# Lower parts of the down-projection weights: one subtraction on VectorE, or a negated copy on ScalarE and an accumulating DMA

## The chip, the cores and the metric

The kernel is one program on one core of a Trainium2 chip. The metric is device microseconds of one execution. The kernel before takes 2463.43 us (median of 3 runs, 2463.13 to 2463.51).

## The reference

Two transformer blocks are computed on the same 512 tokens of width 1024, in float32. The first block has windowed attention and neighbourhood attention side by side, gates, an output projection, and a feed-forward part of width 4096:

```python
h2 = rms_norm(x, norm_mlp[l])
x = x + jnp.square(jax.nn.relu(h2 @ w_up[l])) @ w_down[l]
```

The second block has two layers. Each holds a gated feed-forward part of width 2816, an attention and short-convolution mixer, and a second gated feed-forward part:

```python
def swiglu(h, w_gate, w_up, w_down):
    return (jax.nn.silu(h @ w_gate) * (h @ w_up)) @ w_down
x = x + 0.5 * swiglu(rms_norm_2(x, ffn1_norm[l]), ffn1_wg[l], ffn1_wu[l], ffn1_wd[l])
...
x = x + 0.5 * swiglu(rms_norm_2(x, ffn2_norm[l]), ffn2_wg[l], ffn2_wu[l], ffn2_wd[l])
```

So there are five feed-forward parts: `mlp`, and `ffn1` and `ffn2` of either layer. Each has a down projection (`w_down`, `ffn1_wd`, `ffn2_wd`).

## The kernel before

**Split operands.** Activations are held transposed: 8 tiles of 128 features by 512 tokens. To keep float32 accuracy with TensorE's float32r operands, every matrix is held as an upper part (rounded to float32r) and a lower part (what the rounding left). A product is three matmuls: upper weight by upper activation, upper by lower, lower by upper (lines 450 to 452 for the down projections).

**Weights.** All weights lie in HBM as one stream in the order in which they are used. SyncE loads it in units of up to 1024 columns (512 KB, line 333) into 5 buffers `raw`. The stream is cut into 1282 items. An item is what TensorE needs for one step: at most 128x512 of a weight. `split_item` (line 357) makes an item's two parts: ScalarE writes the upper part `wh` (line 376, CAST), VectorE subtracts it from the raw weight into the lower part `wl` (line 378). Both come from rings of 7 buffers. An item is split five items (`AHEAD`) before the matmuls that use it, in program order, so ScalarE's and VectorE's queues hold these splits between the work on the results of the steps before. When the last item of a unit is split, the next load is put into SyncE's queue; it waits for the last reader of the old unit.

**Feed-forward parts.** `ffn_order` writes out the order. The hidden features are cut into slices (six for `mlp`, of 4, 4, 6, 6, 6 and 6 blocks of 128; four for the others, of 4, 6, 5 and 7). Up projections are steps "P" (seven products of 256 columns, Strassen's scheme, lines 1082 to 1084; their items are a whole 128x512, some of them sums of raw weights made by VectorE at line 355) or "R" (plain, lines 1120 to 1122). Down projections are steps "D" (slice, output block n, part 0 or 1): 16 for each slice. The D steps of one slice stand between the P steps of the next one; those of the last slice stand alone at the end. A D item has the columns of half a slice: 256 (two blocks), 384 (three) or 512 (four). All 352 D items: 96 in `mlp` (32 of 256, 64 of 384), and 64 in each of the other four (24 of 256, 32 of 384, 8 of 512), together 128 of 256, 192 of 384 and 32 of 512.

**After the last D step of an output block** VectorE adds the result to the residual (line 897) and prepares the next part's operands: in `prep_pairs` (line 613) and `squares` (line 572) ScalarE and VectorE take turns, and the next output block queues behind.

**Other queues.** GpSimd's queue issues a few DMAs: constants, 12 bias tables of 384 KB in the attention stage, 8 tiles of 256 KB of the input (line 1037), the last at 325 us.

The items and the split:

Of the kernel before, what the change touches and what calls it, by code (L numbers as in the profile page):

```python
# [9 lines left out]
F32 = mybir.dt.float32  # L10
F32R = mybir.dt.float32r
AF = mybir.ActivationFunctionType
ALU = mybir.AluOpType
# [5 lines left out]
D = 1024  # L19
# [212 lines left out]
def two_blocks(ctx, tc, plan, xT, wstream, vecs, sinks, rpb_g, dists, masks, outT):  # L232
    nc = tc.nc
# [75 lines left out]
    for i in range(4):  # L309
        s = slot[7 * i:7 * i + 7]  # L310
        lo, hi = slice(0, H), slice(H, S)
# [12 lines left out]
    def load_unit():  # L324
        u = st["unit"]
        if u >= len(units):
            return
        st["unit"] += 1
        w = sum(len(b[2]) for b in units[u])
        r = raw_p.tile([P, UNIT], F32, tag="raw", name=f"raw{u}")  # L330
        src = wstream[st["off"]: st["off"] + P * w].rearrange("(p f) -> p f", p=P)
        st["off"] += P * w
        nc.sync.dma_start(r[:, :w], src)
        raw[u] = r

    def parts_of(key, part):
        nk = len(blocks[key][2]) // P
        h = nk // 2
        return (0, h) if part == 0 else (h, nk)

    def combine(idx):

        if idx >= len(items) or idx in combined:
            return
        combined.add(idx)
        key, part = items[idx]
        if key[1:2] == ("P",) and part in (6, 7, 3):
            ra, rb = raw[where[key][0][0]], raw[where[key][1][0]]
            a11, a12, a21, a22 = ra[:, :S], ra[:, S:], rb[:, :S], rb[:, S:]
            new = sums_of.setdefault(key, {})  # L350
            for name, p, q, op in {6: (("s1", a21, a22, ALU.add), ("s2", "s1", a11, ALU.subtract)),
                                   7: (("s3", a11, a21, ALU.subtract),), 3: (("s4", a12, "s2", ALU.subtract),)}[part]:
                new[name] = t = big("t", f"{name}_{idx}")[:, :S]
                p, q = (new[v] if isinstance(v, str) else v for v in (p, q))
                nc.vector.tensor_tensor(t, p, q, op)  # L355

    def split_item(idx):
        key, part = items[idx]
        combine(idx)
        h = wt_p.tile([P, S], F32R, tag="wh", name=f"wh{idx}")  # L360
        lo = wt_p.tile([P, S], F32R, tag="wl", name=f"wl{idx}")
        if blocks[key][0] is not None:
            (u, off), = where[key]
            k0, k1 = parts_of(key, part)
            src = raw[u][:, off + P * k0:off + P * k1]
        else:
            ra, rb = raw[where[key][0][0]], raw[where[key][1][0]]
            new = sums_of.get(key, {})
            if key[1] == "R":
                src = (ra, rb)[part % 2][:, S * (part // 2):S * (part // 2) + S]  # L370
            else:
                src = {1: ra[:, :S], 2: ra[:, S:], 4: rb[:, S:]}.get(part)
                if src is None:
                    src = new[{5: "s1", 6: "s2", 7: "s3", 3: "s4"}[part]]
        w = src.shape[1]
        nc.scalar.copy(h[:, :w], src)  # L376
        combine(idx + 1)
        nc.vector.tensor_tensor(lo[:, :w], src, h[:, :w].bitcast(F32), ALU.subtract)  # L378
        ready[idx] = (h, lo)
        for u, _ in where[key]:  # L380
            uses[u] -= 1
            if uses[u] == 0:
                raw.pop(u)
                freed.append(u)
        while freed and min(freed) == st["oldest"]:
            freed.remove(st["oldest"])
            st["oldest"] += 1
            load_unit()
# [4 lines left out]
    def split_to(idx):  # L393
        oldest = min(live) if live else st["next"]
        idx = min(idx, oldest + RING - 1, len(items) - 1)
        while st["split"] <= idx:
            split_item(st["split"])
            st["split"] += 1
# [150 lines left out]
    def big(tag, name):  # L549
        return at_p.tile([P, 768], F32, tag=tag, name=name)  # L550
# [880 lines left out]
```

## Time and profile before

| | |
|---|---|
| median of 3 runs | 2463.43 us |
| the profiled execution: its time, its span | 2464.76 us, 2463.0 us |
| TensorE (PE) busy | 2436.1 us, 99% |
| VectorE (DVE) busy | 1960.7 us, 80% |
| ScalarE (ACT) busy | 1261.0 us, 51% |
| GpSimd (POOL) busy | 24.6 us, 1% |
| DMA, share of 16 engines taken by the weight queue | 29.0% |

How to read it: the span is what lies between the first and the last instruction, and the time of the run is 1.8 us more. PE is TensorE's matmuls, whose ends are modelled, so that busy time shows gaps but not the speed inside it. DVE, ACT and POOL are VectorE, ScalarE and GpSimd; SP is SyncE, which only issues DMAs. An instruction's idle time in brackets names what released it.

### The profile page before, as it was taken

The page shows a single profiled execution, that of the slowest core. Times are in us where ns is not written, and L with a number is a line of the kernel's source. Part 1 is how long each engine was busy: PE and PEld are TensorE (multiplying, and loading weights), DVE is VectorE, ACT ScalarE, POOL GpSimd, SP SyncE. Part 2 cuts the span into 40 slices and gives each one's busy share as a digit, 9 for nine tenths or more (in the row PEclk, how much of TensorE's full clock was granted, in tenths as well). Part 3 has the DMA queues.
Part 4 walks back from the last instruction along what each step waited for, and adds up shares of the span by engine and source line. Part 5 has one row for each costly group of instructions (what it writes and reads, how often), then busy time and mean ns, then how long its engine had stood idle before and what let it go on. Part 6 is the DMA issues. An engine that isn't in the chain of part 4 may idle for free.

```text
span 2463.0 us, 39488 instructions
## 1 busy us (share of the span) xinstructions
PE 2436.1 (99%) x15098; PEld 2167.0 (88%) x15098; DVE 1960.7 (80%) x3943; ACT 1261.0 (51%) x2744; POOL 24.6 (1%) x37
## 2 busy tenths in 40 slices
PE   8999999999999999999999999999999999999998
PEld 6888888999879999988899999899999878999997
DVE  7778678877679878768798888898887687988885
ACT  5554355544455545544565445665445455654454
POOL 2000000000000000000000000000000000000000
PEclk9999999999999999999999999999999999999999
DMA  4222432233322332332223323323333322233332
GB/s 161 69 92 88 118 114 82 94 101 100 106 85 91 101 115 88 114 95 69 84 80 103 107 99 101 102 93 112 98 104 106 102 69 77 75 107 108 106 94 79
DMA packets 73901, 239.45 MB, mean 97 GB/s; under 512 B 8320, under 2 KB 10384, under 8 KB 73712
## 3 DMA queue, kind: packets, MB, share of 16 engines
q1 hardware_dynamic: 70496, 228.10, 29.0%
q0 software_dynamic: 1776, 7.27, 1.0%
q8 instruction: 118, 1.93, 0.3%
q10 hardware_dynamic: 1440, 1.57, 0.2%
q14 instruction: 71, 0.58, 0.1%
HBM read 234.81 MB, written 2.10 MB: 96 GB/s over the span
## 4 chain that ended last, share of the span: by engine, by line
PE 93%; DVE 5%; ACT 1%; issue 0%; DMA 0%; SPq 0%; DVEq 0%; ACTq 0%
PE X L1084 7%; PE X L1083 7%; PE X L1082 7%; PE YZ L1082 5%; PE YZ L1083 5%; PE YZ L1084 5%; PE mlp_D L451 2%; PE mlp_D L450 2%; PE mlp_D L452 2%; PE 0, 'ffn2'_D L450 2%; PE 1, 'ffn1'_D L450 2%; PE 0, 'ffn1'_D L450 2%; PE 0, 'ffn1'_D L451 2%; PE 0, 'ffn2'_D L451 2%; PE 1, 'ffn1'_D L451 2%; PE 0, 'ffn1'_D L452 2%
## 5 line engine op out<-in xcount | busy, mean ns | idle before, releaser
L378 DVE TENSOR_TENSOR wl<-raw,wh 128x512 fp32r<-128x512 f32 (+2 forms) x890 | 531.7, 609 | 98.3 <-ACT wh L376 91.4
L376 ACT CAST wh<-raw 128x512 fp32r<-128x512 f32 (+2 forms) x890 | 469.6, 555 | 8.4 <-DMA raw<-in_w 2.6
L1082 PE MATMUL X<-r,wh 128*128 128x256 f32 x1568 | 445.2, 284 | 3.8 <-ACT g L1088 3.6
L1084 PE MATMUL X<-r,wl 128*128 128x256 f32 x1568 | 444.0, 283 | 0.0
L1083 PE MATMUL X<-r,wh 128*128 128x256 f32 x1568 | 443.9, 283 | 0.0
L376 ACT CAST wh<-s 128x512 fp32r<-128x512 f32 x392 | 242.7, 620 | 224.6 <-DVE s L355 219.2
L1082 PE MATMUL YZ<-r,wh 128*128 128x256 f32 x1176 | 334.4, 284 | 0.8 <-ACT u L1094 0.8
L1083 PE MATMUL YZ<-r,wh 128*128 128x256 f32 x1176 | 333.3, 283 | 0.0
L1084 PE MATMUL YZ<-r,wl 128*128 128x256 f32 x1176 | 333.2, 283 | 0.0
L378 DVE TENSOR_TENSOR wl<-s,wh 128x512 fp32r<-128x512 f32 x392 | 268.8, 686 | 69.5 <-ACT wh L376 67.6
L1082 PEld LDWEIGHTS X<-r,wh 128*128 128x128 f32 x1568 | 300.1, 191 | 15.2 <-ACT g L1088 4.0
L1083 PEld LDWEIGHTS X<-r,wh 128*128 128x128 f32 x1568 | 300.1, 191 | 10.3 <-issue 1.2
L1084 PEld LDWEIGHTS X<-r,wl 128*128 128x128 f32 x1568 | 300.2, 191 | 0.0
L1082 PEld LDWEIGHTS YZ<-r,wh 128*128 128x128 f32 x1176 | 226.3, 192 | 1.6 <-ACT u L1094 1.4
L1083 PEld LDWEIGHTS YZ<-r,wh 128*128 128x128 f32 x1176 | 226.3, 192 | 0.2 <-issue 0.2
L1084 PEld LDWEIGHTS YZ<-r,wl 128*128 128x128 f32 x1176 | 226.3, 192 | 0.0
L1096 ACT COPY g<-X 128x256 f32<-128x256 f32 x98 | 36.5, 372 | 141.6 <-PE X L1084 141.5
L1097 DVE TENSOR_TENSOR u<-u,g 128x256 f32<-128x256 f32 x98 | 41.6, 424 | 75.8 <-ACT g L1096 75.8
L450 PE MATMUL mlp_D<-r,wh 128*128 128x512 f32 x256 | 100.1, 391 | 0.0
L451 PE MATMUL mlp_D<-r,wh 128*128 128x512 f32 x256 | 100.1, 391 | 0.0
L452 PE MATMUL mlp_D<-r,wl 128*128 128x512 f32 x256 | 99.6, 389 | 0.0
L1092 ACT COPY u<-X 128x256 f32<-128x256 f32 x98 | 36.5, 373 | 101.0 <-PE X L1084 101.0
(429 smaller groups left out, 5258.9 us busy)
## 6 DMA issues: line engine op xcount, KB each, us to landing
raw<-in_w SPq DMA_DIRECT2D x320, 512.0 KB, 3.7
raw<-in_w SPq DMA_DIRECT2D x64, 384.0 KB, 3.5
raw<-in_w SPq DMA_DIRECT2D x32, 448.0 KB, 3.5
raw<-in_w SPq DMA_DIRECT2D x32, 320.0 KB, 2.9
raw<-in_w SPq DMA_DIRECT2D x28, 256.0 KB, 2.6
bb<-in_rpb POOLq DMA_DIRECT2D x12, 384.0 KB, 3.3
xt<-in_x POOLq DMA_DIRECT2D x8, 256.0 KB, 2.9
xt<-in_x SPq DMA_DIRECT2D x1, 1024.0 KB, 12.7
```

Of the source, the lines that this page charges most:

```text
L376: nc.scalar.copy(h[:, :w], src)
L378: nc.vector.tensor_tensor(lo[:, :w], src, h[:, :w].bitcast(F32), ALU.subtract)
L450: nc.tensor.matmul(self.ps, h[:, c], hx, start=(self.n == 1), stop=False)
L451: nc.tensor.matmul(self.ps, h[:, c], lx, start=False, stop=False)
L452: nc.tensor.matmul(self.ps, lo[:, c], hx, start=False, stop=end)
L1082: nc.tensor.matmul(out, h[:, c], hx, start=first, stop=False, skip_group_check=skip)
L1083: nc.tensor.matmul(out, h[:, c], lx, start=False, stop=False, skip_group_check=skip)
L1084: nc.tensor.matmul(out, l[:, c], hx, start=False, stop=(k == 3), skip_group_check=skip)
L1092: nc.scalar.copy(u[:, lo], out)
L1096: nc.scalar.copy(g[:, hi], out)
L1097: nc.vector.tensor_tensor(u[:, hi], u[:, hi], g[:, hi], ALU.add)
```

## The change

For the items of down projections alone, the lower part is made in another way. ScalarE, behind its cast, writes the negative of the upper part into `wl` (an ACTIVATE with Copy and the scale -1). Then a DMA issued by GpSimd adds the raw weight to it in place, element by element. VectorE's subtraction of these 352 items is gone. All other items are split as before.

```diff
         w = src.shape[1]
         nc.scalar.copy(h[:, :w], src)
-        combine(idx + 1)
-        nc.vector.tensor_tensor(lo[:, :w], src, h[:, :w].bitcast(F32), ALU.subtract)
+        if key[1:2] == ("D",):
+
+            nc.scalar.activation(lo[:, :w], h[:, :w].bitcast(F32), AF.Copy, scale=-1.0)
+            nc.gpsimd.dma_start(lo[:, :w].bitcast(F32), src, accum_op=ALU.add)
+            combine(idx + 1)
+        else:
+            combine(idx + 1)
+            nc.vector.tensor_tensor(lo[:, :w], src, h[:, :w].bitcast(F32), ALU.subtract)
```

Line numbers behind the change are larger by 6.

**First place: the first slice of `mlp`, around item 144** (output block 4, part 0; `wh144` and `wl144` are its parts, `X6` and `g4`, `u4` belong to the up projection between). ScalarE's queue before, then now, then GpSimd's queue now:

```order
L376 CAST wh143_4061<-raw64_4016 128x256
L1259 ACTIVATE g4_3881<-g4_3881 128x512
L1260 ACTIVATE u4_3882<-u4_3882 128x512
L376 CAST wh144_4089<-raw64_4016 128x256
L1088 COPY g6_4098<-X6_4097 128x256
L553 CAST r36_124<-g4_3881 128x512
```

```order
L376 CAST wh143_4068<-raw64_4022 128x256
L379 ACTIVATE wl143_4069<-wh143_4068 128x256
L1265 ACTIVATE g4_3882<-g4_3882 128x512
L1266 ACTIVATE u4_3883<-u4_3883 128x512
L376 CAST wh144_4097<-raw64_4022 128x256
L379 ACTIVATE wl144_4098<-wh144_4097 128x256
L1094 COPY g6_4107<-X6_4106 128x256
L559 CAST r36_124<-g4_3882 128x512
```

```order
L380 DMA wl142_4058<-raw64_4022 128x256
L380 DMA wl143_4069<-raw64_4022 128x256
L380 DMA wl144_4098<-raw64_4022 128x256
L380 DMA wl147_4152<-raw64_4022 128x256
L380 DMA wl148_4163<-raw65_4024 128x256
```

Every D cast on ScalarE is followed by a negated copy, ahead of the copies out of PSUM, and GpSimd's queue holds nothing but the accumulating transfers.

**Second place: the end of `mlp`, where its last D items are split between the preparation of the next part** (`xt` is the residual, `mlp_D_5_2` the last slice's result of output block 2, `sqa`, `sqf` the squares). VectorE's queue before and now:

```order
L586 TENSOR_TENSOR inv_140<-inv_140,sqa4_7147 128x512
L586 TENSOR_TENSOR r32_7062<-r32_7062,sqf4_7151 128x512
L378 TENSOR_TENSOR wl317_7156<-raw125_6956,wh317_7155 128x384
L378 TENSOR_TENSOR wl318_7171<-raw127_7025,wh318_7170 128x384
L897 SCALAR_TENSOR_TENSOR xt_87<-mlp_D_5_2_7108,xt_87 128x512
L627 TENSOR_TENSOR xg2_7184<-xt_87 128x256
```

```order
L592 TENSOR_TENSOR inv_140<-inv_140,sqa4_7239 128x512
L592 TENSOR_TENSOR r32_7150<-r32_7150,sqf4_7243 128x512
L903 SCALAR_TENSOR_TENSOR xt_87<-mlp_D_5_2_7198,xt_87 128x512
L633 TENSOR_TENSOR xg2_7278<-xt_87 128x256
```

ScalarE's queue at the same place, before and now:

```order
L577 ACTIVATE sqf4_7151<-xt_87 128x512
L376 CAST wh317_7155<-raw125_6956 128x384
L376 CAST wh318_7170<-raw127_7025 128x384
L626 ACTIVATE r14_102<-xt_87,gfg_153 128x256
L628 ACTIVATE r14_102<-xg2_7184,gfg_153 128x256
```

```order
L583 ACTIVATE sqf4_7243<-xt_87 128x512
L376 CAST wh317_7247<-raw125_7039 128x384
L379 ACTIVATE wl317_7248<-wh317_7247 128x384
L376 CAST wh318_7263<-raw127_7112 128x384
L379 ACTIVATE wl318_7264<-wh318_7263 128x384
L632 ACTIVATE r14_102<-xt_87,gfg_153 128x256
```

The pair of subtractions between two output blocks is gone from VectorE, and ScalarE has four instructions there for two.

## Rows read from the trace of the kernel before

**Rows 1.** The page's first part: busy us, share of the span, instructions.
```profile
PE 2436.1 (99%) x15098; PEld 2167.0 (88%) x15098; DVE 1960.7 (80%) x3943; ACT 1261.0 (51%) x2744; POOL 24.6 (1%) x37
```

**Rows 2.** PE's waits, whole span: us in total, times, longest.
```profile
PE R L1120 <- ACT r L1125: 4.0, 1, 4.0
PE X L1082 <- ACT g L1088: 3.6, 2, 2.8
```

**Rows 3.** Groups by form: count, busy us, mean ns, idle before and releaser.
```profile
L378 DVE TENSOR_TENSOR wl<-raw,wh 128x384 fp32r<-128x384 f32 x192 | 105.3, 553 | 32.3 <-ACT wh L376 32.3
L378 DVE TENSOR_TENSOR wl<-raw,wh 128x256 fp32r<-128x256 f32 x160 | 66.3, 418 | 11.0 <-ACT wh L376 10.5
L376 ACT CAST wh<-raw 128x512 fp32r<-128x512 f32 x538 | 322.1, 617 | 2.7 <-DMA raw<-in_w 2.6
...
L376 ACT CAST wh<-raw 128x384 fp32r<-128x384 f32 x192 | 95.8, 511 | 4.2 <-PE 1, 'ffn2'_D L451 1.0 <-PE 0, 'ffn1'_D L451 1.0 <-PE 1, 'ffn1'_D L451 1.0
L376 ACT CAST wh<-raw 128x256 fp32r<-128x256 f32 x160 | 62.8, 403 | 1.5 <-PE mlp_D L452 1.1 <-PE mlp_D L451 0.4
...
L577 ACT ACTIVATE sqa<-xt 128x512 f32<-128x512 f32 x36 | 22.3, 618 | 7.3 <-DVE xt L897 7.3
```

**Rows 4.** GpSimd's loads: KB and median us to landing, extremes, one issue and its releaser.
```profile
bb<-in_rpb POOLq DMA_DIRECT2D x12, 384.0 KB, 3.3
xt<-in_x POOLq DMA_DIRECT2D x8, 256.0 KB, 2.9
...
DMA to landing us min/median/max: 3.1/3.3/4.2
...
271.08 0.69 DVE L1036 TENSOR_TENSOR gb<-xt,gb 128x512 f32<-128x512 f32 x1
...
272.07 0.54 POOL L1037 DMA_DIRECT2D xt<-in_x  x1 [49.47 <-DVE gb L1036]
```

**Rows 5.** Timeline: start us, us, instruction; three D casts, each with its first lower matmul.
```profile
409.12 0.39 ACT L376 CAST wh<-raw 128x256 fp32r<-128x256 f32 x1
...
413.07 0.39 PE L452 MATMUL mlp_D<-r,wl 128*128 128x512 f32 x1
...
838.02 0.41 ACT L376 CAST wh<-raw 128x256 fp32r<-128x256 f32 x1
...
843.72 0.39 PE L452 MATMUL 0, 'ffn1'_D<-r,wl 128*128 128x512 f32 x1
...
2319.08 0.51 ACT L376 CAST wh<-raw 128x384 fp32r<-128x384 f32 x1
...
2324.26 0.39 PE L452 MATMUL 1, 'ffn2'_D<-r,wl 128*128 128x512 f32 x1
```

**Rows 6.** Timeline, end of `mlp`: the pairs of subtractions; ScalarE between.
```profile
687.79 1.02 DVE L378 TENSOR_TENSOR wl<-raw,wh 128x384 fp32r<-128x384 f32 x2
693.44 1.02 DVE L378 TENSOR_TENSOR wl<-raw,wh 128x384 fp32r<-128x384 f32 x2
...
698.72 1.02 DVE L378 TENSOR_TENSOR wl<-raw,wh 128x384 fp32r<-128x384 f32 x2
...
697.90 0.91 ACT L376 CAST wh<-raw 128x384 fp32r<-128x384 f32 x2
700.37 0.72 ACT L637 ACTIVATE r<-xt,gfg 128x512 fp32r<-128x512 f32 x1 [1.56 <-DVE xt L897]
```

**Rows 7.** Two of PE's stalls, and stretches behind them: busy by engine, PEclk, DMA.
```profile
714.77 0.80 PE L1120 MATMUL R<-r,wh 128*128 128x512 f32 x1 [4.04 <-ACT r L1125]
...
714.70:721.60 6.90, 6.83 (x17) 5.39 (x18) 6.83 (x12) 4.99 (x11) 0.00 (x0) 0.54 0.00 0
...
391.49 0.39 PE L1082 MATMUL X<-r,wh 128*128 128x256 f32 x1 [0.79 <-ACT g L1088]
...
391.40:400.00 8.60, 8.51 (x54) 7.79 (x55) 7.00 (x15) 4.91 (x13) 0.00 (x0) 1.00 0.24 81
```

## The prediction

> **What bounds the kernel now.** I read the page's first part, then TensorE's waits over the whole span, then the costliest groups by form, and last the timeline around down projections. The first part shows PE busy for 2436.1 of 2463.0 us, VectorE for 1960.7 and ScalarE for 1261.0 [rows 1]. A PE at 99% leaves 27 us that a faster VectorE could give back. PE's waits say where they are: no row names the lower weights `wl`, so VectorE's subtractions are in time everywhere. What is worth having is two stalls behind ScalarE: 4.0 us once on the R steps, at the change from `mlp` to `ffn1`, and 3.6 us in two waits on a copy out of PSUM [rows 2]; the rest lies at the start and the end of the program, where no down item is split. So the kernel is bound by TensorE in its D and P steps, and by the exchange between VectorE and ScalarE only at the end of `mlp`.
>
> **What goes.** 352 subtractions: 128 of 256 columns by 418 ns, 192 of 384 by 553 ns [rows 3], and 32 of 512 by some 690 ns (the same 135 ns more for 128 columns more): 53.5 + 106.2 + 22.1 = 182 us of VectorE, 7% of the span. Since TensorE doesn't wait for them, this is worth nothing in itself, except at the end of `mlp`. There three pairs of 1.02 us stand ahead of the next residual add [rows 6], some 0.95 us each until the add starts. The end of `mlp` is a chain: VectorE's add releases ScalarE's preparation, which sat idle 1.56 us for it [rows 6], ScalarE's results release VectorE, and the copy that TensorE waited 4.04 us for is in ScalarE's queue behind all of it [rows 7]. Without the pairs VectorE is 3 x 0.95 = 2.9 us earlier. ScalarE gets six negated copies there, two between two blocks, 2 x 0.51 = 1.0 us by the cast of the same width [rows 3], and they fit into the 1.56 us that it sat idle. But once the adds come earlier it has only about 1.56 - 0.95 = 0.6 us for these 1.0, so it takes back up to 0.4 us a block in the two blocks that follow at once. I take 2.5 us off the stall, which leaves 1.5.
>
> Behind that stall the granted clock was 0.54 for 6.9 us, the lower of its two levels (1.2 of 2.4 GHz) for most of it; PE had stood idle for 4.04 us before it fell. Behind a stall of 0.79 us at 391 it stayed at 1.00 [rows 7]. The low stretch costs 6.9 x 0.46 = 3.2 us. A stall of 1.5 us lies between the two, nearer to the short one, and I take the 3.2 us as given back, with two chances in three.
>
> **What comes on ScalarE.** 352 negated copies. The trace has no activation with a constant scale on these shapes; the nearest, a Square of 512 columns, takes 618 ns where the cast takes 617 [rows 3], so I price them as casts: 128 x 403 + 192 x 511 + 32 x 617 = 169 us, which raises ScalarE from 1261 to 1430 us, 58%. That is beside the matmuls. It can't be a gain, and at worst each copy out of PSUM behind one comes 0.4 to 0.5 us later; TensorE waited for such a copy only twice outside the R steps [rows 2]; the longer wait, 2.8 us, is at the start of `ffn1`, with no D item near. At the other, at 391 [rows 7], a D cast and its copy are now in the queue ahead, and I put 0.5 us there.
>
> **What comes on GpSimd and the DMA engines.** 352 accumulating transfers, 128 of 128 KB, 192 of 192 KB, 32 of 256 KB. One issue took 0.54 us, and started 0.30 us behind the end of the VectorE instruction that released it (272.07 - 271.77) [rows 4]; 190 us of GpSimd, which has nothing else to do. No accumulating transfer is in the trace. From issue to landing GpSimd's loads of 256 KB took 2.9 us and of 384 KB 3.3 us, up to 4.2 [rows 4], so 128 KB more are 0.4 us more. An accumulation reads the raw weights and the destination: twice the bytes. Lower bound: the doubled reads cost nothing, 2.5 us for 128 KB. Upper bound: reading and adding are two passes, one behind the other, 5.0 us for 128 KB and 5.4 for 192. I take the bytes read as what counts, and so the rows for 256 and 384 KB themselves: 2.9 us for 256 columns, 3.3 for 384, 3.7 for 512.
>
> The Trainium skill (Collectives: The Full Stack, "The bandwidth ceiling: the fold count and why AG ≠ RS ≠ AR") says of a reduction in the DMA path that the add itself is free and only its second source read costs, halving the rate. Taken so, the sum is mine; the trace has no accumulation to show it, so it settles nothing about the upper bound.
>
> **Is it in time?** The lead is from the end of a D cast to the first lower matmul of its item. At the tight place it is 413.07 - 409.51 = 3.56 us, at an ordinary one 843.72 - 838.43 = 5.29, and for 384 columns 2324.26 - 2319.59 = 4.67 [rows 5]. Against them stand the negated copy, the start of the issue and the transfer: 0.40 + 0.30 + 2.9 = 3.6 us for 256 columns, 0.51 + 0.30 + 3.3 = 4.1 for 384. So the ordinary places are in time by 1.7 and 0.6 us, and the tightest is level. The tight ones come at the start of a slice. I put 1 us in all for the handful that miss. At the end of `mlp` the casts at 697.90 are later than elsewhere, and TensorE may wait 1 to 2 us there, but it then waits less for ScalarE at 714: no cost.
>
> One more wait is added: the load into a raw buffer (SyncE's queue, in order) now waits for the transfer's landing rather than for the subtraction, some 3 us later for units that D items end. Everything behind it on that queue moves too. The cover is the five buffers: casts lost only 2.6 us to loads in the whole run [rows 3]. I cost it at nothing; without cover it would take from the lead.
>
> The Trainium skill (SBUF — State Buffer, "Who interferes with whom") states that GpSimd's making of descriptors can be blocked by VectorE in its two-port modes, and infers that two-input operations don't block it. By the rule's strict reading each issue would wait for a VectorE operation of 0.4 to 0.7 us, which puts the tight places out of time; no row here shows an issue beside such an operation.
>
> **Sum.** Against the profiled execution (2464.76 us, span 2463.0): - 2.5 (stall) - 3.2 (clock) + 0.5 (copy) + 1.0 (tight places) = - 4.2 us, so 2460.6; the median of the runs shown is 1.3 us below that execution, which gives 2459.3, say 2459.5.
>
> **Rivals.**
> *Tight places pay.* If a transfer takes 4.2 us, the longest of GpSimd's loads [rows 4], the tight place misses by 0.40 + 0.30 + 4.2 - 3.56 = 1.3 us and the 384-column one by 5.0 - 4.67 = 0.3, while the ordinary one still holds by 0.4. 272 D items stand between P steps (five slices of `mlp`, three of each other part, 16 each); if one in eight pays 0.4 us, that is 14 us, less the 4 to be had: 2473. For it: engines shared with weight loads that take 29% of them (the table of the profile), and VectorE at 80% beside the issues. Against it: half of the 384 KB loads landed within 3.3 us.
> *The transfer is two passes, and TensorE waits for it.* At 5.0 and 5.4 us the tight place misses by 2.1 us, the ordinary by 0.4, the 384-column one by 1.5. A miss pushes TensorE back, not ScalarE's casts already done, so the next four or five items have that much more lead: one item in five pays, 272 / 5 = 54, by about 1 us: 2463.4 + 54 = 2517. From some 3.5 us for 128 KB on the loss outweighs the gain. For it: nothing in the trace has an addition in a transfer. Against it: reads can run beside each other, with 16 engines 29% busy.
> *Hidden, and nothing comes back.* ScalarE takes VectorE's place as the pace at the end of `mlp` (its copies are in the chain), the stall stays, the clock falls: 2463.5.
>
> **How the numbers follow.** Forecast 0.50, tight places 0.18, two passes 0.20, nothing 0.12. A measurement of this kernel tells about 0.2% (4.9 us) from no change, so faster means below 2458.5. The forecast's own range is 2456 (the whole 4.0 us and the clock) to 2462 (the stall without the clock); two fifths of its chance are below 2458.5: 0.20, and 0.30 of no change. Tight places give 0.05 of no change and 0.13 of slower, two passes 0.20 of slower, nothing 0.12 of no change. With that, faster 0.20, same 0.45, slower 0.35, of which I move 0.02 to slower for the unknown issue cost of an accumulation. The range is 2456 to 2505: it takes in the tight places and the cheaper half of the two passes.
>
> **What would show it.** Right: no PE wait on a GpSimd transfer outside the starts of slices; transfers of 2.9 to 3.7 us from issue to landing; the 4.04 us wait on L1125 at 1.5 us or less, and no stretch of clock 0.54 behind it; VectorE near 1779 us busy, ScalarE near 1430. Wrong: PE waits named after `wl` all over the D steps, or casts waiting for raw loads. A landing of 4 us or more for 128 KB would make the sign wrong.

## The result and the profile after

The changed kernel takes 2542.51 us (2540.64 to 2550.96, four runs) where the kernel before takes 2463.47 us (2463.13 to 2464.25): a ratio of 1.0327, interval 1.0304 to 1.0350. I had forecast 2459.5 us, in a range from 2456 to 2505. It is slower by 79 us, and outside the range. The profiled execution took 2550.96 us (span 2549.2), 86.2 us of span more than the profiled one of before. Executions differ by their mean granted clock: the four of the kernel after go from 2540.64 us at 0.995 to 2550.96 at 0.991, and of 21 of the kernel before ten at 0.996 took 2463.64 to 2464.98 us and five at 0.998 2462.65 to 2462.81, so both profiled executions are of the slower kind.

The page's first part of the kernel after, as [rows 1]:

```profile
PE 2465.6 (97%) x15098; PEld 2174.1 (85%) x15098; DVE 1819.9 (71%) x3591; ACT 1423.2 (56%) x3096; POOL 331.7 (13%) x389
```

VectorE lost 141 us of work and ScalarE gained 162. PE runs the same 15098 matmuls. Its idle time (span less busy) rose from 26.9 us [rows 1] to 83.6, by 56.7; its busy time rose by 29.5.

PE's waits of the kernel after (us in total, times, longest), as [rows 2], say what it waits for:

```profile
PE 0, 'ffn2'_D L458 <- DMA wl<-raw: 13.9, 9, 2.4
PE 1, 'ffn2'_D L458 <- DMA wl<-raw: 13.2, 8, 2.4
PE 0, 'ffn1'_D L458 <- DMA wl<-raw: 12.7, 9, 2.6
PE 1, 'ffn1'_D L458 <- DMA wl<-raw: 12.0, 10, 2.2
...
PE mlp_D L458 <- DMA wl<-raw: 6.4, 8, 2.2
PE X L1088 <- ACT g L1094: 4.1, 2, 2.8
...
PE R L1126 <- ACT r L1131: 0.9, 2, 0.5
```

The five rows on `wl` are new: 58.2 us in 44 waits, spread over all five parts. The wait on the R steps fell from 4.0 to 0.9 us. So the term that I counted as a gain came, and is buried under a wait that I had priced at 1 us.

The new instructions on the page (count, busy us, mean ns, idle before), the transfers by size with KB and median us from issue to landing, and two lines of the answer on the transfer's line (an issue in ns, then landings in us: least, median, most):

```profile
L380 POOL DMA_DIRECT2D wl<-raw x352 | 306.7, 877 | 1893.6 <-ACT g L1094 647.3
...
L376 ACT CAST wh<-raw 128x512 fp32r<-128x512 f32 (+2 forms) x890 | 474.9, 554 | 8.9 <-DMA raw<-in_w 8.0
...
L379 ACT ACTIVATE wl<-wh 128x256 fp32r<-128x256 f32 (+2 forms) x352 | 174.6, 496 | 11.2
...
wl<-raw POOLq DMA_DIRECT2D x192, 192.0 KB, 3.7
...
wl<-raw POOLq DMA_DIRECT2D x128, 128.0 KB, 2.9
...
wl<-raw POOLq DMA_DIRECT2D x32, 256.0 KB, 4.7
...
L380 POOL DMA_DIRECT2D wl<-raw x352: 860/869/1174, 391.6 to 2524.7; - x176
...
DMA to landing us min/median/max: 2.6/3.7/8.0
```

For 128 KB the median is the one I took (2.9); for 192 and 256 KB it is 0.4 and 1.0 us above mine (3.3, 3.7); the longest is 8.0. The median hides two populations, which the timeline shows. Here is a late transfer of 128 KB in `ffn2` (start us, us, instruction, [idle before <- releaser]; SyncE's row covers two weight loads, issued at 1316.93 and 1318.32):

```profile
1316.87 0.40 ACT L376 CAST wh<-raw 128x256 fp32r<-128x256 f32 x1
...
1316.93 1.71 SPq L333 DMA_DIRECT2D raw<-in_w  x2
...
1317.30 0.42 ACT L379 ACTIVATE wl<-wh 128x256 fp32r<-128x256 f32 x1
...
1318.01 0.87 POOL L380 DMA_DIRECT2D wl<-raw  x1 [4.11 <-ACT u L1100]
...
1321.14 0.40 PE L457 MATMUL 0, 'ffn2'_D<-r,wh 128*128 128x512 f32 x1
...
1323.95 0.50 PE L458 MATMUL 0, 'ffn2'_D<-r,wl 128*128 128x512 f32 x1 [2.41 <-DMA wl<-raw]
```

The cast ended at 1317.27, and PE was ready for the lower weights at 1323.95 - 2.41 = 1321.54: a lead of 4.3 us. The negated copy (0.42) and the start of the issue (1318.01 - 1317.72 = 0.29) are as predicted, and with 2.9 us more all would have been in time by 0.6. But the transfer took 5.9 us. One weight load of 512 KB had been issued 1.1 us before it, and another came 0.3 us behind it. What the DMA engines did meanwhile (queue: packets, MB, share of 16 engines; q1 carries the weight loads, q0 the transfers) in 1317.5 to 1320.5, then 1320.5 to 1322.5, and last, for a transfer issued at 1726.31 with no load beside it, in 1725.5 to 1729.5:

```profile
q1 hardware_dynamic: 174, 0.65, 75.7%
q0 software_dynamic: 12, 0.01, 2.5%
...
q1 hardware_dynamic: 104, 0.39, 55.2%
q0 software_dynamic: 116, 0.11, 35.0%
...
q0 software_dynamic: 144, 0.13, 22.6%
q1 hardware_dynamic: 4, 0.00, 0.1%
...
wl<-raw POOLq DMA_DIRECT2D x1, 128.0 KB, 2.7
```

At 1320.5, 2.5 us behind the issue at 1318.01, the engines had started 12 of the transfer's 144 packets, and the loads took 75.7% of the engines. The transfer's other packets went by turns with the second load's, until 1323. The transfer alone had its first packet 1.4 us behind its issue and had started all 144 by 2.5 us; they took 22.6% of 4 us, 0.9 us, and the landing came at 2.7.

Sorted by whether a weight load could be under way beside it (either counted from 1.7 us behind its issue to its landing), the 352 transfers fall into two groups: 145 without one have a median of 2.98 us (most 4.61), 207 with one a median of 4.71, a quarter over 5.8 and the longest 8.04. This split is worked out from the records of issue and landing; counted from 1.3 us it gives medians of 2.87 and 4.44. The packets' records, taken in the queue's order, show two parts of the delay: those with a load beside have their first packet 2.43 us behind the issue in the median, the others 1.44, and from the first packet to the last it is 1.57 us for 1.19. So such a transfer both starts later and is stretched.

The idle time has a second price. Stretches of the kernel after (busy by engine, PEclk, DMA share, GB/s): behind the stall above, the stretch after that, and the end of `mlp` with the two waits on the R steps in it, where [rows 7] has a clock of 0.54:

```profile
1325.00:1328.40 3.40, 3.40 (x18) 3.40 (x17) 1.30 (x3) 0.00 (x0) 0.00 (x0) 0.51 0.42 151
1328.40:1332.00 3.60, 3.60 (x27) 3.38 (x27) 2.30 (x6) 2.43 (x6) 0.52 (x1) 1.00 0.00 0
...
720.00:735.00 15.00, 13.61 (x57) 10.29 (x57) 14.33 (x26) 10.24 (x21) 0.00 (x0) 1.00 0.34 109
```

For 3.4 us PE is at the lower of its two levels (1.2 of 2.4 GHz) although it has work throughout. There are eleven such new stretches, each behind a wait on `wl` of 1.75 to 2.6 us, while the one at 714 is gone (three waits of 1.78, 2.35 and 2.36 us have none behind them). The mean granted clock of the whole span went from 0.996 to 0.991: 0.009 x 2549.2 - 0.004 x 2463.0 = 13 us. Set against the kernel before matmul by matmul, from start to start (worked out from the timeline), the 86 us of span are 65 at the 44 waits on `wl`, 14 net in stretches of low clock, and 9 at the matmuls just behind the waits and in other D steps, less 2 to 3 at the stalls that both kernels have. The first matmul behind a wait takes 0.50 us for 0.39.

### The profile page after: what moved, and what is told of

Read it like the earlier page. It is cut to its first block, busy times and chain, and to the rows that moved or that the text cites. A ratio compares the mean times of both kernels' runs of the same rounds, so it can differ in the third digit from the quotient of the medians.

```text
span 2549.2 us, 40496 instructions
## 1 busy us (share of the span) xinstructions
PE 2465.6 (97%) x15098; PEld 2174.1 (85%) x15098; DVE 1819.9 (71%) x3591; ACT 1423.2 (56%) x3096; POOL 331.7 (13%) x389
## 3 DMA queue, kind: packets, MB, share of 16 engines
q0 software_dynamic: 52464, 70.20, 16.3%
q10 hardware_dynamic: 1440, 1.57, 0.2%
## 4 chain that ended last, share of the span: by engine, by line
PE 73%; DMA 11%; issue 10%; DVE 2%; ACT 2%; POOL 1%; POOLq 0%; SPq 0%; DVEq 0%; ACTq 0%
DMA wl<-raw 11%; PE X L1088 5%; PE X L1090 5%; PE X L1089 5%; PE YZ L1088 3%; PE YZ L1090 3%; PE YZ L1089 3%; PE 0, 'ffn1'_D L458 1%; PE mlp_D L458 1%; PE 1, 'ffn1'_D L458 1%; PE 0, 'ffn2'_D L458 1%; PE 1, 'ffn2'_D L458 1%; PE 0, 'ffn1'_D L456 1%; PE 0, 'ffn1'_D L457 1%; PE 1, 'ffn1'_D L456 1%
## 5 line engine op out<-in xcount | busy, mean ns | idle before, releaser
L380 POOL DMA_DIRECT2D wl<-raw x352 | 306.7, 877 | 1893.6 <-ACT g L1094 647.3
L376 ACT CAST wh<-raw 128x512 fp32r<-128x512 f32 (+2 forms) x890 | 474.9, 554 | 8.9 <-DMA raw<-in_w 8.0
L384 DVE TENSOR_TENSOR wl<-raw,wh 128x512 fp32r<-128x512 f32 (+1 forms) x538 | 355.0, 671 | 54.4 <-ACT wh L376 48.0
L1088 PEld LDWEIGHTS X<-r,wh 128*128 128x128 f32 x1568 | 304.5, 194 | 16.6 <-ACT g L1094 4.6
L1089 PEld LDWEIGHTS X<-r,wh 128*128 128x128 f32 x1568 | 304.3, 194 | 11.0 <-issue 1.2
L379 ACT ACTIVATE wl<-wh 128x256 fp32r<-128x256 f32 (+2 forms) x352 | 174.6, 496 | 11.2
L1094 ACT COPY g<-X 128x256 f32<-128x256 f32 x98 | 36.3, 370 | 170.7 <-PE X L1090 170.7
L1102 ACT COPY g<-X 128x256 f32<-128x256 f32 x98 | 36.5, 372 | 133.3 <-PE X L1090 133.2
L457 PE MATMUL mlp_D<-r,wh 128*128 128x512 f32 x256 | 100.9, 394 | 0.5 <-DVE r L560 0.5
```

Source lines behind the costliest of these rows:

```text
L379: nc.scalar.activation(lo[:, :w], h[:, :w].bitcast(F32), AF.Copy, scale=-1.0)
L380: nc.gpsimd.dma_start(lo[:, :w].bitcast(F32), src, accum_op=ALU.add)
L457: nc.tensor.matmul(self.ps, h[:, c], lx, start=False, stop=False)
L1088: nc.tensor.matmul(out, h[:, c], hx, start=first, stop=False, skip_group_check=skip)
L1089: nc.tensor.matmul(out, h[:, c], lx, start=False, stop=False, skip_group_check=skip)
L1094: nc.scalar.copy(g[:, lo], out)
```

## Experiments

Theory 1: the transfers land late because weight loads are under way on the same engines. Theory 1a: a load's packets that are already queued are served first; theory 1b: the packets of the two take turns. Theory 2: the addition itself makes them slow, whatever is beside them. Theory 3: ScalarE's added copies push work back. The run named "The end of `mlp` alone" asks whether the predicted gain there is real.

**VectorE adds in place of the transfer.** ScalarE's copies stay, GpSimd's transfers go.

```diff
-            nc.gpsimd.dma_start(lo[:, :w].bitcast(F32), src, accum_op=ALU.add)
+            nc.vector.tensor_tensor(lo[:, :w], src, lo[:, :w].bitcast(F32), ALU.add)
```

> All 352 down items keep ScalarE's negated copy, and VectorE adds the raw weight to it (a two-input operation as long as the subtraction was), so there is no accumulating transfer. Theory 1 (the transfers land late because they queue on the 16 DMA engines behind weight loads) and theory 2 (an accumulation takes long by itself) both expect no wait on the lower weights and 2463 to 2467 us: ScalarE's 170 us more lie beside the matmuls. Theory 3 (not the transfer: the negated copies delay ScalarE's casts and its copies out of PSUM) expects a good part of the 79 us, 2490 us or more.

2471.03 us (2470.22 to 2472.11), ratio 1.0029 [1.0018, 1.0041]. PE's wait on the R steps, and its place in the timeline:

```profile
PE R L1126 <- ACT r L1131: 4.0, 1, 4.0
...
719.37 0.50 PE L1126 MATMUL R<-r,wh 128*128 128x512 f32 x1 [4.05 <-ACT r L1131]
```

No row names `wl`; 71 of the 79 us are gone, so the transfers carry the loss. The rest, 7.3 us over the kernel before as it ran beside this one (2463.77), is more than expected. The R stall has no part in it: it is as long as before, but ends 4.6 us later (719.37 against 714.77 [rows 7]), so most of the rest is collected up to the end of `mlp`. The edit also makes VectorE's addition wait for ScalarE's negated copy and puts it ahead of the call that sums the next item's parts; these were not separated from ScalarE's added time.

**Weight loads cut to 64 columns.** The first five loads are whole, later ones bring only 64 columns into fixed buffers, so the weights are stale; the transfers are as in the changed kernel.

```diff
-        nc.sync.dma_start(r[:, :w], src)
+        w = w if u < RAW_BUFS else 64
+        nc.sync.dma_start(r[:, :w], src[:, :w])
```

> The changed kernel with five fixed raw buffers that are loaded in full once; every later load brings only 64 of up to 1024 columns, so most weights are old ones (left out: the rest of the weight stream). The accumulating transfers are all there. Theory 1 (queueing behind weight loads) expects medians of 2.7, 3.0 and 3.3 us from issue to landing for 128, 192 and 256 KB with hardly any above 4, waits of PE on the lower weights below 5 us where there were 58, no stretches of low clock behind them, and a span of 2455 to 2462 us. Theory 2 (slow by itself) expects the spread of the changed kernel, quartiles up to 4.5 to 5 us, and a span near 2545 us.

2461.77 us in a single run (span 2460.0). Its transfers by size and over all, and PE's wait on the R steps (lines 5 further down):

```profile
wl<-raw POOLq DMA_DIRECT2D x192, 192.0 KB, 3.0
wl<-raw POOLq DMA_DIRECT2D x128, 128.0 KB, 2.7
...
wl<-raw POOLq DMA_DIRECT2D x32, 256.0 KB, 3.5
...
DMA to landing us min/median/max: 2.6/3.0/5.5
...
PE R L1131 <- ACT r L1136: 2.0, 2, 1.5
```

The same 352 additions, and no wait on `wl`: 22 land later than 4 us, against 159 in the changed kernel. Theory 1 holds, and theory 2 alone doesn't. Theory 3 is small here too: with the copies on ScalarE the kernel is not slower than before (though raw weights that come early may help it).

**One item more of lead.** `AHEAD` 6 for 5, in the changed kernel.

```diff
-AHEAD = 5
+AHEAD = 6
```

> The changed kernel with every item split six items ahead and not five, same rings of 7. If the loss is that a transfer's landing misses the lead (theories 1 and 2), one item more, 1.4 to 2 us, covers most of the misses: waits of PE on the lower weights fall from 58 us to 10 to 25, and the time to 2480 to 2500 us. If ScalarE's queue or late raw loads make the loss, earlier splits change little or make it worse: 2535 us or more.

2471.62 us (2470.27 to 2473.03), ratio 1.0031 [1.0019, 1.0043]. Landings, and two of PE's waits:

```profile
DMA to landing us min/median/max: 2.6/4.2/7.6
...
PE X L1088 <- ACT g L1102: 3.2, 5, 1.2
...
PE mlp_D L458 <- DMA wl<-raw: 1.3, 3, 0.8
```

The transfers land later still (median 4.2), and yet PE's waits on `wl` come to 2.8 us, since the lead grew by some 2 us; I had expected 10 to 25 us of waits and 2480 to 2500 us. So the loss is lateness against a deadline, not the engines' throughput. Not all of the distance to before is the transfers', as the next run shows.

**The kernel before with the same lead.** The same one-line edit in the kernel before.

> The kernel before with every item split six items ahead and not five, no other change: the control for the changed kernel with six, which takes 2471.6. If six items ahead cost time by themselves (splits stand ahead of the copies out of PSUM, which TensorE waits for), this takes 2467 to 2470 us; if not, 2463 us, and the 8 us left there are the change's own.

2467.15 us (2466.01 to 2467.98, eleven runs), ratio 1.0014 [1.0005, 1.0023]. One of PE's waits:

```profile
PE X L1082 <- ACT g L1096: 3.2, 5, 1.2
```

The longer lead costs 3.5 us by itself, through ScalarE's copies out of PSUM: the row is the one that stands in the run above. Of that run's 8 us over before, some 4 to 4.5 are left for the change.

**Each weight load in pieces of 256 columns.** As many bytes, in up to four issues.

```diff
-        nc.sync.dma_start(r[:, :w], src)
+        for c in range(0, w, 256):
+            nc.sync.dma_start(r[:, c:min(w, c + 256)], src[:, c:min(w, c + 256)])
```

> The changed kernel with each weight load issued as pieces of 256 columns (up to four DMAs in a row on SyncE's queue), the same bytes. Theory 1a (a load's whole share of an engine's work, some 1.3 us or more, is served ahead of a transfer that comes behind it, so the order of the queues makes it late): a transfer gets in between two pieces, landings above 4 us fall from 159 of 352 to under 80, and the time to 2480 to 2515 us. Theory 1b (the two share the engines packet by packet, and the bytes in flight make it late): landings as before or later, since pieces have rows of 1 KB: 2535 to 2560 us.

2471.88 us (2471.44 to 2473.16), ratio 1.0035 [1.0022, 1.0049]. Loads and transfers by size, and the longer waits on `wl`:

```profile
raw<-in_w SPq DMA_DIRECT2D x1688, 128.0 KB, 2.4
wl<-raw POOLq DMA_DIRECT2D x192, 192.0 KB, 3.6
wl<-raw POOLq DMA_DIRECT2D x128, 128.0 KB, 3.3
wl<-raw POOLq DMA_DIRECT2D x32, 256.0 KB, 4.4
...
PE 0, 'ffn2'_D L459 <- DMA wl<-raw: 2.7, 5, 0.7
...
PE 0, 'ffn1'_D L459 <- DMA wl<-raw: 2.3, 3, 1.1
```

The bytes beside the transfers are the same, and the median of 128 KB is even higher, but the tail is cut: the longest landing is 6.2 us for 8.0, and transfers with a load beside have a median of 4.0 for 4.7. The waits on `wl` are 6.9 us in 11. So not the bytes alone decide. The time is better than theory 1a expected, but landings above 4 us fell from 159 to 115 only, not to under 80. By the packets' records, with a load beside, the first packet comes 1.76 us behind the issue where it was 2.43, as theory 1a has it, while first to last packet stays at 1.67 us for 1.57. The edit also cuts the loads' packets from up to 4096 to 1024 bytes, so a transfer that takes turns with them would start sooner too: theories 1a and 1b are not separated here, although the expectation treated them so. At the start of the program PE waits 2.4 us for a cast, for which the loads now come in four issues, and 2.0 us less in its first wait (6.1 for 8.1).

**A plain transfer.** It overwrites the negated copy with the raw weights; the addition is left out.

```diff
-            nc.gpsimd.dma_start(lo[:, :w].bitcast(F32), src, accum_op=ALU.add)
+            nc.gpsimd.dma_start(lo[:, :w].bitcast(F32), src)
```

> The changed kernel with a plain transfer of the raw weight into the lower buffer in the accumulation's place (left out: the addition, so the lower part is the raw weight). Theory 1 (weight loads ahead on the engines): without a load beside it lands some 0.2 to 0.4 us sooner (half the bytes read), with one still 1 to 3 us later than alone; two thirds or more of the waits on the lower weights stay: 2510 to 2535 us. Theory 2 (the addition is what is slow): the waits go, 2462 to 2475 us.

2477.79 us (2473.76 to 2480.24), ratio 1.0062 [1.0047, 1.0077]. The issues, the landings, and q0 on its page:

```profile
L380 POOL DMA_DIRECT2D wl<-raw x352 | 188.8, 536 | 1933.5 <-ACT g L1094 648.6
...
q0 software_dynamic: 22768, 70.20, 7.7%
...
DMA to landing us min/median/max: 1.9/2.4/5.9
```

I expected two thirds of the waits to stay; 6.7 of 58.2 us did, and the time lies in neither theory's range. The addition has a price of its own: the issue 877 ns for 536, and 16.3% of 2549.2 = 416 us of the engines' time for the same 70.20 MB, against 7.7% of 2472.0 = 190 (7.27 MB of them, some 25 us, are GpSimd's other loads). Sorted as above, the two prices add up. Without a load beside, 128 KB land at 1.96 us plain and 2.69 accumulating, with one at 3.75 and 4.40; for 192 KB it is 2.13 and 3.00, and 3.86 and 4.85. So the addition costs 0.65 to 1.0 us and a load beside 1.7 to 1.9, each with the other or without it. Theory 1 needs its rival's half: a transfer misses the usual lead by much only with both, and without the load the kernel takes 2461.77 us, without the addition 2477.79. What in the addition costs (the longer issue, the second read, the shorter packets) is not separated.

**The end of `mlp` alone.** Only the 16 items of `mlp`'s last slice take the new path.

```diff
-        if key[1:2] == ("D",):
+        if key[:2] == ("mlp", "D") and key[2] == len(SLICES1) - 1:
```

> Only the 16 down items of the last slice of mlp are made with the negated copy and the transfer; all others with the subtraction. By the part of the prediction on the end of mlp: the wait of 4.0 us on the R steps falls to about 1 us, the stretch of low clock behind it (3.2 us) goes, no other stall comes: 2457 us, 6 us faster than before. If the end of mlp gains nothing by itself: 2463 us; if the 16 transfers are late there, a stall of 1 to 3 us on the lower weights and 2460 to 2466 us.

2461.51 us (2461.07 to 2461.76, eleven runs), ratio 0.9991 [0.9982, 1.0000]. PE's waits:

```profile
PE R L1126 <- ACT r L1131: 1.4, 2, 0.9
PE X L1088 <- ACT u L1098: 1.4, 1, 1.4
```

The R wait is 1.4 us, where the prediction left 1.5, and the clock doesn't fall at 714. Of the 5.7 us that it added up, 2.3 reached the time and, profile against profile, 3.7 the span. A new wait of 1.4 us behind ScalarE takes some back.

**The last slice of each part.** 80 items, 16 in each of the five parts.

```diff
-        if key[1:2] == ("D",):
+        if key[1:2] == ("D",) and key[2] == len(SLICES1 if key[0] == "mlp" else SLICES2) - 1:
```

> The accumulating transfer only for the 80 down items in the last slice of each feed-forward part, where the items stand alone and the leads shown are 6 us and more. If lateness against the lead makes the loss, none comes here, and mlp's end gives its 2 to 3 us as in the run with that slice alone: 2460 to 2462 us. If each transfer costs in another way, 80 of 352 take their share: 2475 us or more.

2461.19 us (2460.55 to 2461.37, eleven runs), ratio 0.9990 [0.9982, 0.9999]: 2.4 us under before, the fastest kernel that computes the reference, by about what these runs can just tell. Its transfers, landings, the R wait, and its only wait on `wl`:

```profile
wl<-raw POOLq DMA_DIRECT2D x48, 192.0 KB, 4.1
wl<-raw POOLq DMA_DIRECT2D x32, 256.0 KB, 4.3
...
DMA to landing us min/median/max: 3.0/4.2/7.5
...
PE R L1126 <- ACT r L1131: 1.3, 2, 0.9
...
PE mlp_D L458 <- DMA wl<-raw: 0.3, 1, 0.3
```

Its transfers are as late as any, up to 7.5 us, and PE waits 0.3 us in all for them: worked out from the timeline, the lead of these 80 items is 9.3 us in the median, that of the other 272 in the changed kernel 5.9. There 43 of the 44 waits on `wl` fall on these 272. So the loss sits with the items that stand between P steps. The 64 items beyond `mlp`'s gain nothing over the run before, which fits the statement that PE never waited for their subtractions.

## Why the prediction was wrong

- **VectorE's subtractions are worth nothing except at the end of `mlp`: right.** VectorE's busy time fell by 141 us and that brings nothing elsewhere. I had counted 182 us, the sum of the subtractions' durations; in the trace VectorE's instructions overlap their neighbours (a pair of 0.55 us each takes 1.02 [rows 6]), so busy time fell by less, to 1819.9 us and not 1779. The R wait came out at 0.9 us (forecast 1.5 or less), and the stretch of 0.54 behind it is gone.
- **ScalarE's copies at the cast's price: right** (174.6 us against 169), and the start of the transfer's issue behind them too (0.29 against 0.30). The 0.5 us for the copy at 391 came as well (4.1 us for 3.6 on that row of PE's waits). I had read two waits on copies out of PSUM there; four shorter ones of 0.2 to 0.3 us stand beside them, and nothing hangs on it.
- **GpSimd's issue at 0.54 us: wrong.** The accumulating issue takes 0.87, the plain one 0.54. The row that I used was a plain load.
- **Transfers at 2.9, 3.3 and 3.7 us, and with them the 1.0 us for tight places in the sum: the step that failed.** Alone they land even earlier (2.7, 3.0 and 3.5 with small loads beside). I took these durations from GpSimd's loads [rows 4] and set them against leads of 3.6 to 5.3 us [rows 5] as if they held at every place. But 207 of 352 transfers have a weight load beside and take 4.7 us in the median. The loads recur with the D items, since an item's raw buffer, once its transfer has landed, is free for the next load (SyncE's loads waited 815.9 us in all for such landings, 168 times). I had the engines' 29% share of loads in hand, named it for one rival and read it as room against the other; it is an average, and in the stretch shown it was 75.7%. The 44 waits fell on items with leads of 3.6 to 6.7 us, so not at the tight places alone. That turns "1 us for the handful that miss" into 58.2 us of waits, and with what follows them into the whole loss.
- **The rivals had the right shape and a wrong size.** "Two passes" has one item in five paying about 1 us, 54 us in all; 44 waits came to 58.2. Its mechanism was half right: the addition does double the engines' time, but alone it adds 0.7 to 0.9 us to a landing of 128 or 192 KB, and it takes a load's packets beside it to miss the deadline by much. It stopped at 2517 us because it left out the clock, some 14 us behind the stalls, and the slower matmuls there, some 9. Yet [rows 7] showed a stall of 4 us and the low level behind it. With both it would have been near 2540. The range ended at 2505 since I cut that rival in half.
- **The sign to watch, a landing of 4 us for 128 KB:** the median of 128 KB was 2.9, so read on medians the condition didn't hold, and the sign was wrong all the same. The condition should have been put on the slow quarter.
- **The load's longer wait for its raw buffer at nothing:** ScalarE's casts lost 8.0 us to raw loads, before 2.6 [rows 3]; small beside the rest, as costed.

The Trainium skill (Collectives: The Full Stack, "The bandwidth ceiling: the fold count and why AG ≠ RS ≠ AR") has the second source read halve the rate. The engines' time, 416 us against 190, agrees. The sum was wrong although it followed that rule, because a rate says little of a landing beside another queue's packets. The Trainium skill's other rule (SBUF — State Buffer, "Who interferes with whom") would have shown as issues that stretch by a VectorE operation of 0.4 to 0.7 us; they stay at 860 to 869 ns up to the median, 1174 at most, with VectorE 71% busy, so no sign of it here.

Left open: whether a load beside makes a transfer late by standing ahead of it or by taking turns with it; and which part of the 4 to 7.3 us that the change still costs, when the transfers are in time or on VectorE, belongs to ScalarE's copies and which to the order around them.

## What to carry to other kernels

When work moves from an engine to a DMA, price the transfer by its slow quarter with the neighbours that it will have, and set that against the shortest leads: here medians that fit all but the tightest leads still cost 79 us. A mean share of the DMA engines says nothing of the microsecond in which the transfer is issued; look at what is issued just before and just behind it. And a stall on TensorE can cost more than its length: behind most of those of about 2 us there was a stretch at the lower clock here.

## What was not expected of the hardware

An accumulating transfer between SBUF buffers costs GpSimd 869 ns to issue, a plain one 536. It moves one packet a row (144 for 128 rows here, 50688 for the 352 transfers; q0's 52464 holds 1776 of other loads), the plain one 20992 for the same bytes. Beside two 512 KB loads it had 12 of its 144 packets started 2.5 us behind its issue, where one alone had all, and cutting the loads into pieces of 128 KB brings the longest landing from 8.0 to 6.2 us. Behind eleven waits of TensorE of 1.75 to 2.6 us the granted clock was near 0.5 for 3.4 us; behind one of 0.79 us it was not [rows 7], nor behind three of 1.78, 2.35 and 2.36 us.
